# The end of a decoder block's FFN: the last token tile in two column pieces, its norm's sums in three parts

## The chip, the cores and the metric

One core of a Trainium2 chip runs the whole kernel in one launch. The metric is the device time in microseconds, median of three runs. TensorE multiplies, VectorE (DVE in the profile) and ScalarE (ACT) do the elementwise work, GpSimd (POOL) a part of it, and SyncE (SP) issues every DMA from one queue, in order.

## The reference, cut to what matters

One decoder layer on 1024 tokens and 16 meta tokens, model width 1024, in float32: a norm, a wide input projection, three mixers, a gated merge, a residual, a SwiGLU FFN of width 2816, a residual, and a final norm over each token.

```python
for l in range(DEPTH):
    u = rms_norm(h, norm_mix[l])
    proj = u @ w_in[l]
    ...
    g = jax.nn.sigmoid(gates).reshape(b, t, N_BRANCH, D_MODEL)
    merged = (g[:, :, 0] * (o_a @ w_branch[l, 0])
              + g[:, :, 1] * (o_f @ w_branch[l, 1])
              + g[:, :, 2] * (o_c @ w_branch[l, 2]))
    h = h + merged @ w_out[l]
    u = rms_norm(h, norm_ffn[l])
    gate_ff, up_ff = jnp.split(u @ w_ffn_in[l], 2, axis=-1)
    h = h + (jax.nn.silu(gate_ff) * up_ff) @ w_ffn_out[l]
return rms_norm(h, norm_final)[:, N_META:]
```

`rms_norm(y)` is y times the gain, divided by the root of the mean of y squared over the 1024 columns plus 1e-6.

## The kernel before, in words

Every product is made of three TensorE multiplies: an operand is split into a high and a low part, and high by high, high by low and low by high are summed in a PSUM bank. A full multiply moves 512 columns over a 128 by 128 weight tile.

The stages run in this order. The normalised input lies feature by feature in the four `u` tiles `uh0`, `ul0`, `uh1`, `ul1` (L210). The projections multiply weight tiles with them, and the mixers run in between. The 24 gate tiles (`gate`, L733) come from the same projections: for each of them TensorE makes two halves of 512 tokens, the second from `uh1` and `ul1`, ScalarE copies each half to a `z` tile, and a DMA writes that to DRAM (`gz`). The mixers' outputs lie in DRAM too (`osp`). After the last gate the `u` tiles are given up. The branch stage (L800 to L828) then multiplies the mixer outputs with the branch weights. It holds 24 tiles of 4096 bytes a partition, `oA`, `oC` and `oF` (all named `o4` in the program), loaded by `load_o` (L773). `oA` and `oC`, 16 tiles in the pool `r3`, are used first, in turns; `oF`, 8 tiles in the pool `b4`, is used only from L848 on. The branch weights (`wb`) and the gates (`sg`) are fetched two steps ahead (`fetch`, L777). Branch products are named `mm_br`, projections `mm_w`.

SBUF is filled from two sides. The pools `const`, `wstream` and `z` stand at the left side, in this order, and the `u` pool behind them; the pools of a stage stand at the right side. A tile that takes the place of an earlier one waits until the last reader of the earlier one is done. `const` is filled up with a `pad` of 192 bytes (L72) so that what follows starts at a multiple of 512 bytes. In the program as built, `ul1` takes the bytes 101888 to 118272 of each partition, and the first `oA` tile, `o4_1421`, starts at 118272.

Python code states the work; a scheduler then sets the order on each engine by a model of when things are ready, keeping what depends on what. TensorE runs its rows in order, and SP issues its DMAs in order: a DMA that waits holds back all that stand behind it.

The FFN's second product is cut into seven block products (a Strassen-like scheme, `product2(i, banks, ...)`, L1139), each over 11 operand pairs `ab` of 128 by 512, for four token tiles x of 128 tokens. The last one, `product2(6, yb, False, last)` at L1209, loads all 11 pairs and then goes token tile by token tile. After each tile, `last(x)` adds the PSUM bank to the residual `ho[4 + x][0]` (DVE), `total` squares and sums it (ACT, `Square` with an accumulator, into `sums`), and `finish` makes the reciprocal root (`rstd_from`, L176: a DVE `tensor_scalar` on the first column, an ACT `Sqrt` on the last one, a DVE reciprocal), multiplies both halves by it and by the gain `gfc` (DVE) and writes them out.

```python
def rstd_from(q, n):
    ...
    first = q[:n, 0:1]
    if q.shape[-1] > 2:
        tc.keep_in_program_order(dve.tensor_tensor(r[:n], first, q[:n, 1:2], ALU.add))
        first = r[:n]
    dve.tensor_scalar(e[:n], first, 1.0 / D, EPS, ALU.mult, ALU.add)
    act.activation(r[:n], q[:n, -1:], AF.Sqrt, bias=e[:n], scale=1.0 / D)
    dve.reciprocal(r[:n], r[:n])
```

Of the kernel before, what the change touches and what calls it, by code (L numbers as in the profile page):

```python
# [9 lines left out]
F32 = mybir.dt.float32  # L10
F32R = mybir.dt.float32r
AF = mybir.ActivationFunctionType
ALU = mybir.AluOpType
# [3 lines left out]
P = 128  # L17
# [34 lines left out]
def hybrid_block(ctx, tc, h_in, w_in, w_v0, w_v1, w_bd, par, rows, gains, relt, onehot,  # L52
                 maskrow, cmask, w_br, w_out, w_fi, w_fo, out):
    nc = tc.nc
    act, dve, pool, pe = nc.scalar, nc.vector, nc.gpsimd, nc.tensor

    def dma(dst, src):
        nc.sync.dma_start(f32(dst) if dst.dtype == F32R else dst, f32(src) if src.dtype == F32R else src)
# [7 lines left out]
    cp = ctx.enter_context(tc.tile_pool(name="const", bufs=1, side="left"))  # L66
# [12 lines left out]
    def nm(s):  # L79
        uid[0] += 1  # L80
        return f"{s}_{uid[0]}"
# [94 lines left out]
    def rstd_from(q, n):  # L176

        e = cp.tile([P, 1], F32, tag="re", bufs=4, name=nm("re"))
        r = cp.tile([P, 1], F32, tag="rs", bufs=4, name=nm("rs"))
# [7 lines that stand above are left out]
        return r  # L187

    def rstd_of(x, n, junk):

        q = cp.tile([P, 2], F32, tag="sq2", bufs=4, name=nm("sq"))
        for i in range(2):
            act.activation(junk[i], x[i], AF.Square, accum_out=q[:n, i:i + 1])
        return rstd_from(q, n)

    def halves(x):
        return x[:, :512], x[:, 512:]
# [633 lines left out]
    with tc.tile_pool(name="r4", bufs=1, side="right", reuse_waits="tile") as r4:  # L831
# [26 lines left out]
        with tc.tile_pool(name="r4b", bufs=1, side="right", reuse_waits="tile") as r4b:  # L858
            for c in range(2):
                u2[c] = [pair_tile(mp if c else bp) for k in range(KT // 2)]  # L860
                for tt in range(4 * c, 4 * c + 4):
# [3 lines left out]
                    q = slice(t0, t0 + P)  # L865
# [8 lines left out]
                    r = rstd_of(halves(ht), P, halves(xg))  # L874
# [20 lines left out]
    NJ = NF // 2  # L895
# [6 lines left out]
    def add(eng, o, a, b):  # L902
        eng.tensor_tensor(o, a, b, ALU.add)

    with tc.tile_pool(name="r5", bufs=1, side="right", reuse_waits="tile") as r5:
        def t5(tag, bufs, n=512):
            return r5.tile([P, n], F32, tag=tag, bufs=bufs, name=nm(tag))
# [6 lines left out]
        def operand(pl, tag, bufs, src):  # L914
            t = pl.tile([P, 2, 512], F32R, tag=tag, bufs=bufs, name=nm(tag))
            split(t[:, 0], t[:, 1], src)
            return t

        def swiglu_plain(f):
            w = [load_w(w_fi[f + NF * i], D) for i in range(2)]  # L920
            at_ = []
            for c in range(2):
                pg, pv = (mm_bank(f"_{x}{f}") for x in "gu")
                for ps, (wh, wl) in zip((pg, pv), w):
                    run(mm3(ps, [(wh[:, k * P:(k + 1) * P], wl[:, k * P:(k + 1) * P],
                                  u2[c][k // 2][0][:, k % 2], u2[c][k // 2][1][:, k % 2]) for k in range(KT)]))
                sg = t5("a", 6)
                act.activation(sg, pg, AF.Sigmoid)
                dve.tensor_tensor(sg, pg, sg, ALU.mult)
                dve.tensor_tensor(sg, pv, sg, ALU.mult)  # L930
                at_.append(sg)
            return at_

        def fetch_fi(f, i):
            w = []
            for s in range(2):
                pl = wp if i % 2 else r5
                raw = pl.tile([P, D], F32, tag="wr", bufs=2, name=nm("wr"))
                dma(raw, w_fi[f + NF * s])
                w.append(halves(raw))  # L940
            return w
# [124 lines left out]
        for j in range(NJ):  # L1066
            if j == 0:
                first, second = swiglu_plain(0), swiglu_plain(NJ)
                bb, last, rest = combine()
                spill(0, j, first[0])  # L1070
            elif j == 1:
# [3 lines left out]
                with behind(*last)():  # L1075
                    ops = [t5("s2", 2)] + [operand(r5, "ar", 3, a) for a in (a11, a12)]
# [8 lines left out]
                    ops = [t5("s2", 2), operand(wp, "wh", 2, a11), operand(wp, "wl", 2, a12)]  # L1085
# [7 lines left out]
                first = first_  # L1093
                spill(0, j, first[0])
                second, _ = swiglu(1 + NJ, w_, bb, None, ops, behind(*mark))
            else:
                with tc.issue_after(seen):
                    first, _ = swiglu(j, fetch_fi(j, 0), bb, pool)
# [13 lines left out]
    with (tc.tile_pool(name="ring0", bufs=4, side="right", reuse_waits="tile") as r7,  # L1112
          tc.tile_pool(name="ring1", bufs=10, side="right", reuse_waits="tile") as r8,
          tc.tile_pool(name="r6", bufs=1, side="right", reuse_waits="tile") as r6):
        def h_tile(tt, half):
            t = r6.tile([P, 512], F32, name=f"h{tt}{half}")
            dma(t, h1s[tt, :, 512 * half:512 * half + 512])
            return t

        def right_operand(i, j):  # L1120
            if i in bsp:
                return bsp[i][j]
            row, half = {0: (j, 0), 1: (j + NJ, 0), 5: (j + NJ, 1)}[i]
            return w_fo[row * P:(row + 1) * P, 512 * half:512 * half + 512]

        ring = [0]

        def operands(i, j):

            raw = wp.tile([P, 2, 512], F32, tag=("wr", "wh", "wl")[j % 3], bufs=2, name=nm("raw"))  # L1130
            dma(raw[:, 0], asp[i][j])
            dma(raw[:, 1], right_operand(i, j))
            pl = r7 if ring[0] % 14 < 4 else r8
            ring[0] += 1
            t = pl.tile([P, 2, 2, 512], F32R, tag="ab", name=nm("ab"))
            split(t[:, 0], t[:, 1], raw)
            return t[:, 0], t[:, 1]

        def product2(i, banks, first=True, by_token=None):  # L1139
            def mm(x, ops, js):  # L1140
                q = slice(x * P, (x + 1) * P)
                n = 3 * len(js)
                c = 0
                for j in js:
                    hi, lo = ops[j]
                    for a, b in ((hi, hi), (hi, lo), (lo, hi)):
                        pe.matmul(banks[x], a[:, 0, q], b[:, 1], start=first and j == 0 and c == 0,  # L1147
                                  stop=j == NJ - 1 and c % 3 == 2, skip_group_check=True)
                        c += 1
            if by_token is None:  # L1150
                for j in range(NJ):
                    ops = {j: operands(i, j)}
                    for x in range(4):
                        mm(x, ops, [j])
            else:
                ops = [operands(i, j) for j in range(NJ)]
                for x in range(4):
                    mm(x, ops, range(NJ))
                    by_token(x)

        xb = [mm_bank("_x0"), mm_bank("_x1"), mm_bank("_x2"), o_bank("_x3")]
        yb = [sc_bank("_y0"), sc_bank("_y1"), tr_bank("_y2"), tr_bank("_y3")]
        sums = cp.tile([P, 8, 2], F32, name="sums")

        def total(tt, half):

            o = ho[tt][half]
            junk = r6.tile([P, 512], F32, tag="jk", bufs=2, name=nm("jk"))
            act.activation(junk, o, AF.Square, accum_out=sums[:, tt, half:half + 1])

        def finish(tt):
            r = rstd_from(sums[:, tt], P)
            for half in range(2):
                sl = slice(512 * half, 512 * half + 512)
                o = ho[tt][half]
                dve.scalar_tensor_tensor(o, o, r, gfc[:, sl], ALU.mult, ALU.mult)
                dma(out[tt * P:(tt + 1) * P, sl], o)

        product2(0, yb)
        gfc = r6.tile([P, D], F32, name="gfc")  # L1180
        dma(gfc, gains[1:2].partition_broadcast(P))
        ho = [[h_tile(tt, half) for half in range(2)] for tt in range(8)]
        for x in range(4):
            add(dve, ho[x][0], yb[x], ho[x][0])
        product2(1, xb)
        for x in range(4):
            add(dve, ho[x][0], xb[x], ho[x][0])
            total(x, 0)
        product2(2, yb, False)
        for x in range(4):  # L1190
            add(dve, ho[x][1], yb[x], ho[x][1])
        product2(3, xb)
        for x in range(4):
            add(dve, ho[4 + x][1], xb[x], ho[4 + x][1])
        product2(4, yb, False)
        for x in range(4):
            add(dve, ho[4 + x][1], yb[x], ho[4 + x][1])
            total(4 + x, 1)
        product2(5, xb, False)
        for x in range(4):  # L1200
            add(dve, ho[x][1], xb[x], ho[x][1])
            total(x, 1)
            finish(x)

        def last(x):
            add(dve, ho[4 + x][0], yb[x], ho[4 + x][0])
            total(4 + x, 0)
            finish(4 + x)
        product2(6, yb, False, last)  # L1209

# [72 lines left out]
```

## Time and profile before

| | us |
|---|---|
| median of 3 runs | 1650.19 (1649.83 to 1652.05) |
| the profiled execution, its own time | 1652.01 |
| its span, first to last instruction | 1650.2 |
| TensorE busy | 1627.5 (99%) |
| VectorE busy | 1006.8 (61%) |
| ScalarE busy | 759.7 (46%) |
| GpSimd busy | 389.4 (24%) |
| granted TensorE clock, mean | 0.999 |

The profile shows one execution. Times count from the start of the span. A row of the timeline or of the chain of waits has the start, the duration, the engine, the line and what it works on; "xN" is the number of instructions that were merged. PEld is TensorE's weight load, SPq the queue of SP. Multiplies overlap in their pipeline, so the distance between starts tells their rate, not the duration of one.

### The profile page before, as it was taken

Reading aid. Unit: us, or ns where it says so; the run is one execution under the profiler, and the core shown is the slowest. Engines: PE = TensorE matmul, PEld = TensorE weight load, DVE = VectorE, ACT = ScalarE, POOL = GpSimd, SP = SyncE. Lnnn points to the kernel's source line nnn. Section 1 sums busy time; section 2 is a strip of 40 time slices with the busy share of each in tenths; the row PEclk is TensorE's granted clock in tenths of the full one; section 3 lists DMA queues with packets and bytes.
Section 4 is the critical chain, followed back from the end, with each engine's and each line's share of the span. In section 5 each row is a group of like instructions: output and inputs, shape, how many; then the busy total and the mean of one; then the engine's idle time right before and its main releaser. Section 6 shows DMA issues by size and latency. Waiting matters only on the chain.

```text
span 1650.2 us, 22634 instructions
## 1 busy us (share of the span) xinstructions
PE 1627.5 (99%) x8159; PEld 1372.3 (83%) x8159; DVE 1006.8 (61%) x1815; ACT 759.7 (46%) x1397; POOL 389.4 (24%) x322
## 2 busy tenths in 40 slices
PE   7999999999999999999999999999999999999998
PEld 6899978888888888888887888888888788888886
DVE  6566566555566666651338446977776777466554
ACT  6466466555555555542335443433333343355342
POOL 2000001011122221110224100267765667300000
PEclk9999999999999999999999999999999999999999
DMA  7222342223324142329747221344554444698632
GB/s 254 78 103 94 131 139 77 95 82 122 108 75 129 63 123 73 115 98 318 252 142 230 96 90 70 127 156 172 198 202 148 147 149 151 214 359 275 191 128 102
DMA packets 110880, 242.48 MB, mean 147 GB/s; under 512 B 11944, under 2 KB 23544, under 8 KB 110512
## 3 DMA queue, kind: packets, MB, share of 16 engines
q1 hardware_dynamic: 110768, 241.04, 43.0%
q8 instruction: 64, 1.05, 0.3%
q14 instruction: 48, 0.39, 0.1%
HBM read 163.45 MB, written 72.21 MB: 143 GB/s over the span
## 4 chain that ended last, share of the span: by engine, by line
PE 81%; DVE 6%; DMA 4%; POOL 3%; issue 3%; ACT 2%; SPq 0%; DVEq 0%; POOLq 0%; ACTq 0%
PE mm_w L151 27%; PE mm_s L151 7%; PE mm_br L151 6%; PE mm_wo L151 5%; PE mm_x L1147 4%; PE mm_v L151 4%; PE tr_s L151 4%; PE tr_y L1147 4%; PE sc_y L1147 4%; PE ob L547 4%; PE tr L558 3%; DMA wr<-w_fi_dram 2%; PE sc_s L151 2%; PE ob_x L1147 1%; PE mm_g L151 1%
## 5 line engine op out<-in xcount | busy, mean ns | idle before, releaser
L151 PE MATMUL mm_w<-uh,wh 128*128 128x512 f32 (+2 forms) x744 | 292.6, 393 | 0.0
L151 PE MATMUL mm_w<-uh,wl 128*128 128x512 f32 (+2 forms) x744 | 280.6, 377 | 0.0
L151 PE MATMUL mm_w<-ul,wh 128*128 128x512 f32 (+2 forms) x744 | 279.9, 376 | 0.0
L151 PEld LDWEIGHTS mm_w<-uh,wl 128*128 128x128 f32 x744 | 140.0, 188 | 25.7
L151 PEld LDWEIGHTS mm_w<-uh,wh 128*128 128x128 f32 x744 | 140.4, 189 | 12.8
L151 PEld LDWEIGHTS mm_w<-ul,wh 128*128 128x128 f32 x744 | 140.7, 189 | 11.7
L119 DVE TENSOR_TENSOR ab<-raw,ab 128x1024 fp32r<-128x1024 f32 x77 | 92.9, 1223 | 71.5 <-ACT ab L118 62.0
L118 ACT ACTIVATE wh<-wr 128x1024 fp32r<-128x1024 f32 (+1 forms) x84 | 72.0, 858 | 125.3 <-PE mm_w L151 52.3
L118 ACT ACTIVATE ab<-raw 128x1024 fp32r<-128x1024 f32 x77 | 80.8, 1059 | 95.0 <-PE ob_x L1147 21.4
L151 PE MATMUL mm_s<-pt,ar 128*128 128x512 f32 x492 | 118.8, 390 | 0.8 <-ACT c L954 0.7
L151 PE MATMUL mm_br<-o,wh 128*128 128x512 f32 x384 | 118.3, 389 | 0.0
L119 DVE TENSOR_TENSOR pl<-tr,ph 128x384 fp32r<-128x384 f32 (+2 forms) x160 | 87.4, 555 | 46.9 <-ACT ph L118 42.7
L151 PEld LDWEIGHTS mm_s<-pt,ar 128*128 128x128 f32 x492 | 92.0, 188 | 21.5 <-ACT c L968 1.3
L118 ACT ACTIVATE ph<-tr 128x384 fp32r<-128x384 f32 (+2 forms) x160 | 77.0, 486 | 52.9 <-PE tr L558 50.9
L119 DVE TENSOR_TENSOR wl<-wr,wh 128x1024 fp32r<-128x1024 f32 x45 | 55.8, 1241 | 73.4 <-ACT wh L118 73.1
L648 POOL TENSOR_SCALAR s<-s,sm 128x144 f32<-128x144 f32 (+3 forms) x64 | 48.8, 765 | 171.0 <-DVE sm L647 138.1
L151 PEld LDWEIGHTS mm_br<-o,wh 128*128 128x128 f32 x384 | 72.1, 188 | 14.8
L558 PE MATMUL tr<-ident,s 128*128 128x128 f32 x480 | 79.6, 274 | 1.2 <-POOL s L596 0.6
L151 PE MATMUL mm_wo<-woh,hl 128*128 128x512 f32 x256 | 79.1, 389 | 0.0
L151 PE MATMUL mm_br<-o,wl 128*128 128x512 f32 x192 | 75.2, 392 | 1.5 <-DVE wl L119 1.5
L558 PEld LDWEIGHTS tr<-ident,s 128*128 128x128 f32 x480 | 59.1, 140 | 18.3 <-DVE pl L119 3.4
L1147 PE MATMUL mm_x<-ab 128*128 128x512 f32 x297 | 72.7, 389 | 0.0
(258 smaller groups left out, 3651.9 us busy)
## 6 DMA issues: line engine op xcount, KB each, us to landing
wr<-w_in_dram SPq DMA_DIRECT2D x45, 512.0 KB, 3.6
wr<-w_fi_dram SPq DMA_DIRECT2D x44, 512.0 KB, 4.1
raw<-asp SPq DMA_DIRECT2D x77, 256.0 KB, 3.3
asp<-a SPq DMA_DIRECT2D x66, 256.0 KB, 2.8
gz<-z SPq DMA_DIRECT2D x48, 256.0 KB, 2.0
o<-osp SPq DMA_DIRECT2D x24, 512.0 KB, 5.9
sg<-gz SPq DMA_DIRECT2D x48, 256.0 KB, 3.5
fo<-w_fo_dram SPq DMA_DIRECT2D x22, 512.0 KB, 4.5
```

The source lines that it names most:

```text
L118: a = act.activation(hi, src, AF.Copy)
L119: i = dve.tensor_tensor(lo, src, f32(hi), ALU.subtract)
L151: pe.matmul(ps, a, b, start=first and i == 0, stop=i == n - 1, skip_group_check=not first)
L547: pe.matmul(ob[:, q0:q0 + b - a], vt[:, c], x[:, a:b], start=count == 0, stop=count == n_mm - 1, skip_group_check=True)
L558: pe.transpose(tb[:, col:col + P], src, ident)
L648: pool.tensor_scalar(s[:, :nk], s[:, :nk], den, 1.0, ALU.mult, ALU.mult)
L1147: pe.matmul(banks[x], a[:, 0, q], b[:, 1], start=first and j == 0 and c == 0, stop=j == NJ - 1 and c % 3 == 2, skip_group_check=True)
```

## The change

The last token tile (x = 3) of the last block product is made in two pieces of 256 columns: 33 multiplies for columns 0 to 255, then 33 for columns 256 to 511. `last` runs after each piece on its columns. The sums of squares of a token are kept in three columns of `sums` where two were: the half that was finished earlier, piece 0 (or the full tile for x < 3) and piece 1; the earlier half is now column 0, so that `tensor_scalar` no longer reads the last sum. For x = 3 the second half of the output is multiplied by the gain beforehand (`scaled`, a new tile and a DVE instruction before the last product) and then by the reciprocal root on ScalarE (`Copy` with a scale), while DVE does the first half.

```diff
-                    mm(x, ops, range(NJ))
-                    by_token(x)
+                    for cols in PIECES if x == 3 else ((0, 512),):
+                        mm(x, ops, range(NJ), slice(*cols))
+                        by_token(x, slice(*cols))
...
-        sums = cp.tile([P, 8, 2], F32, name="sums")
+        sums = cp.tile([P, 8, 3], F32, name="sums")
+        PIECES = ((0, 256), (256, 512))
...
-            act.activation(junk, o, AF.Square, accum_out=sums[:, tt, half:half + 1])
+            act.activation(junk[:, cols], o[:, cols], AF.Square, accum_out=sums[:, tt, i:i + 1])
...
-            r = rstd_from(sums[:, tt], P)
+            r = rstd_from(sums[:, tt, :2 if scaled is None else 3], P)
...
-                dve.scalar_tensor_tensor(o, o, r, gfc[:, sl], ALU.mult, ALU.mult)
+                if half and scaled is not None:
+                    o = scaled
+                    act.activation(o, o, AF.Copy, scale=r)
+                else:
+                    dve.scalar_tensor_tensor(o, o, r, gfc[:, sl], ALU.mult, ALU.mult)
...
+        scaled = r6.tile([P, 512], F32, name="scaled")
+        dve.tensor_tensor(scaled, ho[7][1], gfc[:, 512:], ALU.mult)
```

`sums` lies in the pool `const`. It grows from 64 to 96 bytes a partition, and every left pool behind it moves by 32 bytes: in the program as built, `ul1` now takes 101920 to 118304, while `o4_1421` still starts at 118272. The two share 32 bytes.

The rows of SP between the mixers and the branch stage change with it. `z_1397` to `z_1420` are the halves of the last gates, `wr_1414` the last projection weights, `o4_1421` to `o4_1436` `oA` and `oC`, `o4_1437` to `o4_1444` `oF`, `wor` weights of the output product. Before, SP has there, from the last projection weights on:

```order
L58 DMA wr_1414_7761<-w_in_dram 128x1024
L58 DMA o4_1421_7836<-osp_94 128x1024
L58 DMA gz_92<-z_1397_7606 128x512
L58 DMA o4_1425_7840<-osp_94 128x1024
L58 DMA o4_1422_7837<-osp_94 128x1024
L58 DMA o4_1426_7841<-osp_94 128x1024
L58 DMA gz_92<-z_1399_7634 128x512
```

The first tile of `oA` stands right behind the last projection weights, and the others follow among the writes of the gates; the sixteenth, `o4_1436`, and the first branch weights, `wb_1445`, stand ahead of the write of `z_1418`. Now SP has at the same place:

```order
L58 DMA wr_1414_7761<-w_in_dram 128x1024
L58 DMA o4_1437_7852<-osp_94 128x1024
L58 DMA gz_92<-z_1397_7606 128x512
L58 DMA o4_1441_7856<-osp_94 128x1024
L58 DMA o4_1438_7853<-osp_94 128x1024
L58 DMA o4_1442_7857<-osp_94 128x1024
L58 DMA gz_92<-z_1399_7634 128x512
```

The tiles of `oF` have moved to where `oA` was. `oA` now stands around the last two writes of the gates:

```order
L58 DMA gz_92<-z_1413_7758 128x512
L58 DMA gz_92<-z_1418_7792 128x512
L58 DMA o4_1421_7836<-osp_94 128x1024
L58 DMA gz_92<-z_1420_7820 128x512
L58 DMA o4_1425_7840<-osp_94 128x1024
L58 DMA o4_1422_7837<-osp_94 128x1024
L58 DMA o4_1426_7841<-osp_94 128x1024
```

All 16 tiles of `oA` and `oC` have moved behind the write of `z_1418`, and 15 of them behind that of the very last half, `z_1420`. The branch weights follow them directly, here with the last three tiles of `oC` (`o4_1435`, `o4_1432`, `o4_1436`):

```order
L58 DMA o4_1435_7850<-osp_94 128x1024
L58 DMA o4_1432_7847<-osp_94 128x1024
L58 DMA o4_1436_7851<-osp_94 128x1024
L58 DMA wb_1445_7876<-w_br_dram 128x512
L58 DMA sg_1446_7878<-gz_92 128x512
L58 DMA sg_1447_7879<-gz_92 128x512
```

The weights have moved with the tiles: nothing of the branch stage's first step is ahead of `z_1418` any more. TensorE's and DVE's rows between the mixers and the branch stage are the same in both.

At the end of the program ScalarE now has, from the third token tile's sum on (`jk` is scrap, `rs` the reciprocal root, `h70` and `scaled` the two halves of the last tile):

```order
L1172 ACTIVATE jk_2373_14510,sums_13011<-h60_13236 128x512
L185 ACTIVATE rs_2375_14513<-sums_13011,re_2374_14512 128x1
L1172 ACTIVATE jk_2376_14555,sums_13011<-h70_13240 128x256
L1172 ACTIVATE jk_2377_14591,sums_13011<-h70_13240 128x256
L185 ACTIVATE rs_2379_14594<-sums_13011,re_2378_14593 128x1
L1181 ACTIVATE scaled_14318<-scaled_14318,rs_2379_14594 128x512
```

Where one sum of 512 columns stood, two of 256 stand, and the scaling of the second half is last; no table load stands among them.

More of the change, by code (lines that the diff above doesn't have):

```diff
@@ L1139, in product2, with mm @@
         def product2(i, banks, first=True, by_token=None):
-            def mm(x, ops, js):
+            def mm(x, ops, js, cols=slice(0, 512)):
                 q = slice(x * P, (x + 1) * P)
@@ L1146, in mm @@
                     for a, b in ((hi, hi), (hi, lo), (lo, hi)):
-                        pe.matmul(banks[x], a[:, 0, q], b[:, 1], start=first and j == 0 and c == 0,
+                        pe.matmul(banks[x][:, cols], a[:, 0, q], b[:, 1, cols], start=first and j == 0 and c == 0,
                                   stop=j == NJ - 1 and c % 3 == 2, skip_group_check=True)
@@ L1157, in product2, with total, finish @@
                 for x in range(4):
-                    mm(x, ops, range(NJ))
-                    by_token(x)
+                    for cols in PIECES if x == 3 else ((0, 512),):
+                        mm(x, ops, range(NJ), slice(*cols))
+                        by_token(x, slice(*cols))
         xb = [mm_bank("_x0"), mm_bank("_x1"), mm_bank("_x2"), o_bank("_x3")]
         yb = [sc_bank("_y0"), sc_bank("_y1"), tr_bank("_y2"), tr_bank("_y3")]
-        sums = cp.tile([P, 8, 2], F32, name="sums")
-        def total(tt, half):
+        sums = cp.tile([P, 8, 3], F32, name="sums")
+        PIECES = ((0, 256), (256, 512))
+        def total(tt, half, i, cols=slice(0, 512)):
             o = ho[tt][half]
             junk = r6.tile([P, 512], F32, tag="jk", bufs=2, name=nm("jk"))
-            act.activation(junk, o, AF.Square, accum_out=sums[:, tt, half:half + 1])
-        def finish(tt):
-            r = rstd_from(sums[:, tt], P)
+            act.activation(junk[:, cols], o[:, cols], AF.Square, accum_out=sums[:, tt, i:i + 1])
+        def finish(tt, scaled=None):
+            r = rstd_from(sums[:, tt, :2 if scaled is None else 3], P)
             for half in range(2):
@@ L1187, in hybrid_block @@
             add(dve, ho[x][0], xb[x], ho[x][0])
-            total(x, 0)
+            total(x, 0, 0)
         product2(2, yb, False)
@@ L1197, in hybrid_block @@
             add(dve, ho[4 + x][1], yb[x], ho[4 + x][1])
-            total(4 + x, 1)
+            total(4 + x, 1, 0)
         product2(5, xb, False)
@@ L1201, in hybrid_block, with last @@
             add(dve, ho[x][1], xb[x], ho[x][1])
-            total(x, 1)
+            total(x, 1, 1)
             finish(x)
[L1205 to L1208, printed above, removed]
+        scaled = r6.tile([P, 512], F32, name="scaled")
+        dve.tensor_tensor(scaled, ho[7][1], gfc[:, 512:], ALU.mult)
+        def last(x, cols):
+            add(dve, ho[4 + x][0][:, cols], yb[x][:, cols], ho[4 + x][0][:, cols])
+            total(4 + x, 0, 2 if cols.start else 1, cols)
+            if cols.stop == 512:
+                finish(4 + x, scaled if x == 3 else None)
         product2(6, yb, False, last)
```

## The prediction

> **What bounds the kernel now.** The page's busy times come first.
>
> ```profile
> PE 1627.5 (99%) x8159; PEld 1372.3 (83%) x8159; DVE 1006.8 (61%) x1815; ACT 759.7 (46%) x1397; POOL 389.4 (24%) x322
> ```
>
> TensorE is busy for 99% of the span, so a microsecond is won where TensorE isn't running, and lost where it is made to wait. The change is aimed at the stretch behind TensorE's last multiply. The timeline from 1643.4 us on:
>
> ```profile
> 1643.48 0.69 DVE L903 TENSOR_TENSOR h<-tr_y,h 128x512 f32<-128x512 f32 x1 [3.81 <-PE tr_y L1147]
> 1644.26 0.63 ACT L1169 ACTIVATE jk<-h 128x512 f32<-128x512 f32 x1 [6.24 <-DVE h L903]
> 1644.80 0.19 ACT L1169 ACTIVATION_READ_ACCUMULATOR jk<-h 128x1 f32 x1
> 1645.02 0.15 DVE L184 TENSOR_SCALAR re<-sums 128x1 f32<-128x1 f32 x1 [0.85 <-ACT jk L1169]
> 1645.21 0.29 ACT L185 ACTIVATE rs<-sums,re 128x1 f32<-128x1 f32 x1 [0.22 <-DVE re L184]
> 1645.53 0.16 DVE L186 RECIPROCAL rs<-rs 128x1 f32<-128x1 f32 x1 [0.36 <-ACT rs L185]
> 1645.73 1.42 DVE L1176 SCALAR_TENSOR_TENSOR h<-h,rs,gfc 128x512 f32<-128x512 f32 x2
> 1646.51 0.99 SPq L58 DMA_DIRECT2D out_dram<-h  x2
> ```
>
> It is one chain: add, square, offset, root, reciprocal, two scalings, two writes. From 1643.48 to the span's end are 6.7 us; that is all that the end can ever give. The order rows show a second place, the start of the branch stage, so I read the chain of waits there:
>
> ```profile
> 732.52 0.96 PE ob L547 x8
> ...
> 734.41 42.88 PE mm_w L151 x189
> 777.30 86.83 PE mm_br L151 x383
> ```
>
> The last projections (`mm_w`) go over into the first branch products (`mm_br`) at 777.30 without a gap, 383 of them without a wait. The SP queue's timeline shows why:
>
> ```profile
> 738.03 0.40 SPq L58 DMA_DIRECT2D o<-osp  x1
> ...
> 767.49 0.43 SPq L58 DMA_DIRECT2D o<-osp  x1
> 767.97 0.44 SPq L58 DMA_DIRECT2D wb<-w_br_dram  x1
> ```
>
> Between the first and the last of these `o` rows lie all 16 tiles of `oA` and `oC`, and the first branch weights follow at 767.97. ScalarE has those at 774.37, 2.9 us before they are needed:
>
> ```profile
> 774.37 0.63 ACT L118 ACTIVATE wh<-wb 128x512 fp32r<-128x512 f32 x1 [1.83 <-DMA wb<-w_br_dram]
> ```
>
> **The start of the branch stage, where I expect the change to be decided.** `sums` is 32 bytes larger, and `ul1` now overlaps `o4_1421`. That tile's load must wait for the last reader of `ul1`, the last `mm_w`, done at 777.30. In SP's order the other 15 loads, `wb_1445` and the gates' `sg` stand behind it, so nothing of the first step is in SBUF when TensorE wants to begin. TensorE's own rows are unchanged: `mm_br` is next, and nothing can fill the gap. The sizes:
>
> ```profile
> gz<-z SPq DMA_DIRECT2D x48, 256.0 KB, 2.0
> o<-osp SPq DMA_DIRECT2D x24, 512.0 KB, 5.9
> ...
> wb<-w_br_dram SPq DMA_DIRECT2D x24, 256.0 KB, 3.6
> ```
>
> From 777.30 to the first weights, 16 x 512 KB, the last gate write of 256 KB and 256 KB of weights go through: 8.5 MiB, 8.91 MB. For the rate I have the window in which the same loads ran before, and the densest run of loads, 13 of 256 KB (3.41 MB):
>
> ```profile
> 738.00:748.00 10.00, 10.00 (x46) 8.29 (x45) 1.23 (x1) 2.14 (x3) 0.00 (x0) 1.00 0.97 345
> ```
>
> ```profile
> 1444.18 8.44 SPq L58 DMA_DIRECT2D h<-h1s  x13
> ```
>
> The first gives 345 GB/s at a DMA share of 0.97, so 356 at a full share; the second 3.41 MB in 8.44 us, 404 GB/s. I take 356, since it is the same tiles: 25.0 us. The ends are 22.1 us (404) and 27.9 us (320, some 7% under the row, for gate reads in between). [...]
>
> To this come the landing of a transfer in an empty queue, 2.0 us by the `gz` row, and after the weights' landing ScalarE's `wh` (0.63 us by its row) and the weight load (0.19 by the row below), with some 0.05 of semaphores: 2.9 us. So `mm_br` begins at 777.30 + 25.0 + 2.9 = 805.2. Before, by the distance of 0.23 between multiplies, the first began at about 777.1: a delay of 28.1 us. What covered these loads before was 39 us of projections (738.03 to 777.30); what runs under them now is nothing.
>
> Does TensorE resume at full speed? The start of the kernel shows how it behaves after idling:
>
> ```profile
> 9.28 1.94 PE L205 MATMUL tr<-ident,xg 128*128 128x128 f32 x8 [9.28 <-DVE xg L302]
> ...
> 18.21 0.43 PE L151 MATMUL mm_w<-uh,x0h 128*128 128x272 f32 x1
> 18.44 0.43 PE L151 MATMUL mm_w<-ul,x0h 128*128 128x272 f32 x1
> ...
> 19.62 0.29 PE L151 MATMUL mm_w<-ul,x0h 128*128 128x272 f32 x1
> 19.75 0.28 PE L151 MATMUL mm_w<-uh,x0l 128*128 128x272 f32 x1
> ```
>
> ```profile
> 15.68 5.10 PE mm_w L151 x25
> ```
>
> ```profile
> 16.00:18.00 2.00, 2.00 (x10) 1.77 (x10) 1.13 (x4) 1.97 (x5) 1.57 (x1) 1.00 0.82 246
> ```
>
> The granted clock reads 1.00 throughout, yet equal multiplies stand 0.23 us apart until about 19.4 and 0.125 apart after it. By the clock column resuming costs nothing; by the spacing, 3.8 us of dense work (15.68 to about 19.5) lose 45%, 1.7 us. I take 1.7; ends 0 and 4.5 (10 us, counted from 9.28). [...]
>
> Of this delay little can come back, since TensorE hardly waits later in this stage:
>
> ```profile
> PE mm_br L151 <- DVE wl L119: 1.5, 4, 0.6
> ```
>
> At most 1.5 us; I take 0. That `oF` and `wor` come earlier costs nothing: they take `oA`'s old places, with fewer bytes.
>
> **The end.** Terms, by form:
>
> ```profile
> L118 ACT ACTIVATE ph<-tr 128x512 fp32r<-128x512 f32 x64 | 38.0, 594 | 17.5 <-PE tr L558 16.1 <-ACT z L736 0.7
> ...
> L118 ACT ACTIVATE ph<-tr 128x256 fp32r<-128x256 f32 x32 | 12.2, 380 | 18.6 <-PE tr L558 18.5
> ```
>
> ```profile
> L119 DVE TENSOR_TENSOR pl<-tr,ph 128x256 fp32r<-128x256 f32 x32 | 13.5, 423 | 7.8 <-ACT ph L118 4.5 <-DMA osp<-pl 2.6
> ```
>
> ```profile
> L547 PEld LDWEIGHTS ob<-ph,v 128*128 128x128 f32 x272 | 51.2, 188 | 6.7 <-ACT ph L118 1.8
> ```
>
> - The pieces: 66 multiplies of 256 columns with a weight load each; the eight `ob` of that size above took 0.96, 0.12 each: 7.92 us against 33 x 0.227 (86.83/383) = 7.48. +0.44.
> - The add on 256 columns: 0.42 against 0.69. -0.27.
> - `Square`: ScalarE saves 594 - 380 ns from 512 to 256 columns. -0.21.
> - The offset's row (1645.02 to 1645.21) leaves the path. -0.19. Its two small DVE steps run under the last `Square` and its read (some 0.6 us); without that cover they cost 2 x 0.17, gaps included.
> - Both halves are scaled at once. The second write was issued at 1647.17 (1646.51 + 0.99 - 0.33), 1.48 after the reciprocal's end; now ScalarE is done some 0.69 after it, its write takes 0.33, and the other stands behind: 1.06. -0.42.
>
> Together -0.65, between -1.2 and, if none of the shortened steps helps, +0.5. The added gain product is one more DVE step while DVE is 61% busy; it hides under the last product.
>
> **The sum.** 28.1 + 1.7 - 0.65 = 29.1 us on the span of 1650.2. The profiled execution took 1652.01, its span 1650.2; the median of 1650.19 equals the span, so I put the sum on it: 1679.3. Least: 22.1 for 25.0, no slow clock, 1.5 back, -1.2 at the end: 1672.7. Most: 27.9, 4.5, +0.5: 1686.1.
>
> **The rivals.**
> - *The loads are hidden anyway*, and only the end counts: 1649.5, so not slower. It decides if the 16 loads are issued before 777.3 - 27.9 = 749.4. For it: before, SP had the last one out at 767.5. Against: the order rows put 15 behind the write of `z_1420`, which the last `mm_w` feeds. 0.05.
> - *The shift by 32 bytes slows transfers as well.* The stream tiles no longer start at multiples of 512 bytes. [...] No row before shows a shifted stream tile. 0.05.
> - *The pieces are bound by their weight loads*: 66 x 0.188 = 12.4, 4.5 more: 1683.8. Against it the eight `ob`, with equal loads, at 0.12. 0.02.
> - *The end isn't shortened* (ScalarE's scaling comes late): 1680.0. 0.03.
>
> **How the numbers follow.** My forecast has 0.85, at 1679.3. The last three rivals lie in its range; only the first falls out. I give 1673 to 1686. A measurement can tell about 0.2%, 3.3 us: the first rival is "same", 0.05; faster needs more than the end saves, 0.01; slower 0.94.
>
> **What would show it.** TensorE idle from 777.3 to about 805, ended by ScalarE's `wh` behind `wb`; `o` loads at 777 to 790; slow multiplies for some 4 us after that; then the old pace. At the end, 7.9 us for the last tile and writes 1.06 us after the reciprocal. A gap under 20 us, or none, would prove me wrong.

## The result and the profile after

The changed kernel takes 1690.14 us (median, 1688.43 to 1692.74) beside 1650.05 us for the kernel before (four runs of each): a ratio of 1.0236, 95% interval 1.0221 to 1.0251, or 40.1 us more. The prediction had 1679.3, with a range up to 1686: the direction and the place were right, the size was not. The profiled execution took 1689.88 us, its span 1688.1; the mean granted clock fell from 0.999 to 0.991. The two spans differ by 37.9 us, less than the medians, since the profiled execution of the kernel before took 1652.01 us, more than its median.

I read the profile in the order of the prediction. The branch stage first; the chain of waits there, around the one large gap:

```profile
734.05 42.90 PE mm_w L151 x189
777.02 0.61 ACT z L736
777.65 0.32 SPq L58
...
782.35 10.20 DMA o<-osp
792.57 9.37 DMA wb<-w_br_dram
802.02 0.64 ACT wh L118
802.70 91.38 PE mm_br L151 x383
```

The projections no longer go over into the branch products. The chain leaves TensorE at 777.02, goes through ScalarE's last gate half, SP, the loads of `o` and the first branch weights, and comes back at 802.70. SP's timeline shows the loads where the order rows had put them, one ahead of the last gate write and 15 behind it, and that write waits for ScalarE's copy:

```profile
776.74 0.32 SPq L58 DMA_DIRECT2D o<-osp  x1
777.65 0.32 SPq L58 DMA_DIRECT2D gz<-z  x1
778.02 13.62 SPq L58 DMA_DIRECT2D o<-osp  x15
792.57 0.33 SPq L58 DMA_DIRECT2D wb<-w_br_dram  x1
```

The list of waits gives the price, in total, number of times and longest:

```profile
PE mm_br L151 <- ACT wh L118: 25.8, 1, 25.8
```

And the windows of the gap (busy times of the five engines, then the granted clock, the DMA share and the rate) show nothing but DMA, at up to 420 GB/s, until TensorE resumes in the third:

```profile
778.00:788.00 10.00, 0.00 (x0) 0.00 (x0) 0.00 (x0) 0.00 (x0) 0.00 (x0) 0.56 0.95 354
788.00:798.00 10.00, 0.00 (x0) 0.00 (x0) 0.00 (x0) 0.00 (x0) 0.00 (x0) 0.50 1.03 420
798.00:808.00 10.00, 5.30 (x15) 4.22 (x16) 1.85 (x3) 4.62 (x7) 0.00 (x0) 0.57 0.91 331
```

So far the prediction holds. What it did not hold is in the row of the chain that starts at 802.70: the same 383 multiplies that took 86.83 us take 91.38, and the slow clock explains only 1.9 of the 4.5 (below). In the FFN, 300 us after the gap, the groups of 12 multiplies stand in the chain like this:

```profile
1104.42 2.80 PE sc_s L151 x12
1107.23 2.80 PE mm_s L151 x12
1110.02 2.80 PE tr_s L151 x12
```

In the kernel before such a group stood there like this:

```profile
1052.71 2.72 PE sc_s L151 x12
```

That is 12 x 0.2267. At 2.80 it is 0.2333 us a multiply, and TensorE waits for nobody there. That is the first thing the prediction had no term for.

The second is at the end, in the timeline from the second piece on:

```profile
1677.32 4.21 PE L1147 MATMUL tr_y<-ab 128*128 128x256 f32 x33 [0.52 <-DVE h L903]
...
1681.56 0.42 DVE L903 TENSOR_TENSOR h<-tr_y,h 128x256 f32<-128x256 f32 x1 [4.30 <-PE tr_y L1147]
...
1682.02 0.42 ACT L1172 ACTIVATE jk<-h 128x256 f32<-128x256 f32 x1 [4.21 <-DVE h L903]
...
1682.89 0.17 DVE L186 RECIPROCAL rs<-rs 128x1 f32<-128x1 f32 x1 [0.65 <-ACT rs L185]
1683.09 0.72 ACT L1181 ACTIVATE scaled<-scaled,rs 128x512 f32<-128x512 f32 x1 [0.23 <-DVE rs L186]
1683.09 0.75 DVE L1183 SCALAR_TENSOR_TENSOR h<-h,rs,gfc 128x512 f32<-128x512 f32 x1
1683.84 0.33 SPq L58 DMA_DIRECT2D out_dram<-scaled  x1
1684.59 0.33 SPq L58 DMA_DIRECT2D out_dram<-h  x1
```

The second piece waits 0.52 us for DVE's addition of the first one. From the last multiply to the reciprocal it is then 0.72 us shorter than before (from the last multiply's end to the reciprocal's, 1.53 beside 2.25).

### The profile page after: what moved, and what is told of

It reads as the page before. It is cut to its first block, busy times and chain, and to the rows that moved or that the text cites. A ratio compares the mean times of both kernels' runs of the same rounds, so it can differ in the third digit from the quotient of the medians.

```text
span 1688.1 us, 22691 instructions
## 1 busy us (share of the span) xinstructions
PE 1641.6 (97%) x8192; PEld 1375.9 (82%) x8192; DVE 979.3 (58%) x1817; ACT 763.5 (45%) x1400; POOL 384.7 (23%) x322
## 4 chain that ended last, share of the span: by engine, by line
PE 90%; DVE 3%; ACT 2%; DMA 2%; issue 1%; SPq 0%; POOL 0%; ACTq 0%; DVEq 0%; POOLq 0%
PE mm_w L151 27%; PE mm_s L151 13%; PE tr_s L151 7%; PE mm_br L151 6%; PE mm_wo L151 5%; PE mm_x L1147 4%; PE mm_v L151 4%; PE tr_y L1147 4%; PE sc_y L1147 4%; PE sc_s L151 3%; PE ob L547 3%; PE tr L558 3%; PE ob_x L1147 1%; PE mm_g L151 1%; PE mm_u L151 1%
## 5 line engine op out<-in xcount | busy, mean ns | idle before, releaser
L151 PEld LDWEIGHTS mm_w<-uh,wh 128*128 128x128 f32 x744 | 140.4, 189 | 12.8
L151 PEld LDWEIGHTS mm_w<-ul,wh 128*128 128x128 f32 x744 | 140.7, 189 | 11.8
L151 PE MATMUL mm_br<-o,wh 128*128 128x512 f32 x384 | 122.2, 400 | 25.8 <-ACT wh L118 25.8
```

Of the source, the lines that this page charges most:

```text
L151: pe.matmul(ps, a, b, start=first and i == 0, stop=i == n - 1, skip_group_check=not first)
```

## The experiments

Three theories went in. **T1** is the prediction's sum: stall, cold clock (TensorE's slow multiplies right after it has idled), then the old pace. **T2** is what the trace suggests: besides those, a multiply is slower where its two operands lie in tiles of which only one has moved by 32 bytes (left-hand pools moved, right-hand pools did not), and the end loses by the wait between the pieces. **T3** is the rival for the pace: the idle stretch or its low clock leaves TensorE slower for the rest of the run, whatever the addresses.

### The end alone

```diff
 (the changed kernel)
-    pad(cp, 192)
+    pad(cp, 160)
```

> The changed kernel with its left-hand pools 32 bytes lower (the filler of const 160 instead of 192 bytes), so that every pool behind const lies where it lay before the change: no overlap, no moved loads, and what is left of the change is its end. T1 (the prediction's sum: the stall and the cold clock, then the old pace, and an end of -0.65) expects 1649.4 us. T2 (the stall, the cold clock, a slower pace wherever one operand of a multiply lies 32 bytes off the other, and an end that loses because the second piece waits for the addition of the first) expects the trace's end again: second piece 0.5 us after the first, 8.7 instead of 7.5 us for the twelve-times-two multiplies and more of the last token tile, 0.7 us less from the last multiply to the reciprocal; +0.5 us, or 1.0 if the last write again lands late: 1650.6 to 1651.1. T3 (the slower pace is a lasting trace of the idle stretch or of its clock, whatever the addresses) says of this run what T2 says.

Measured: 1651.12 us, ratio 1.0006 [0.9997, 1.0016], so 0.9 us more, and no difference is within the interval. The gap at the branch stage is gone. By the total alone T1's 1649.4 lies just outside; the trace decides. Its chain ahead of the end and the end's wait:

```profile
1611.21 14.96 PE sc_y L1147 x66
1626.17 11.44 PE tr_y L1147 x66
1637.64 0.43 DVE h L903
1638.12 4.22 PE tr_y L1147 x33
```

```profile
PE tr_y L1147 <- DVE h L903: 0.5, 1, 0.5
```

In the kernel before:

```profile
1613.52 14.96 PE sc_y L1147 x66
1628.48 14.97 PE tr_y L1147 x66
```

So the pieces end 31.14 us after the start of the last `sc_y` multiplies (1611.21 to 1642.35), where the kernel before took 29.94 (1613.52 to 1643.46): +1.20. From the last multiply's end to the span's end it is 5.95 instead of 6.74: 0.79 come back. T2's account of the end stands: +0.4 by the trace. What follows from this run is more than that: with 32 bytes taken from a filler, nearly all of the 40 us is gone.

### The stall alone

```diff
 (the kernel before)
-    with tc.tile_pool(name="r3", bufs=16, side="right", reuse_waits="tile") as r3:
+    with (tc.tile_pool(name="gap", bufs=1, side="right") as gap,
+          tc.tile_pool(name="r3", bufs=16, side="right", reuse_waits="tile") as r3):
+        gap.tile([P, 128], F32, name="gap512")
```

> The kernel before with a 512-byte filler ahead of the pool r3 of the branch stage: its last tile of o comes to overlap the end of ul, as in the changed kernel, and SP's loads stand in the changed kernel's order, but every operand keeps its place within 512 bytes. T1 and T2: stall 25.6 and cold clock 1.9 as the trace of the changed kernel has them, 1677.6 us (1676.5 to 1679), and behind the first ten or so multiplies of the branch stage a multiply each 0.2267 us, 383 of mm_br in about 88.8 us. T3: the slow pace comes with the idle stretch, so 0.2333 us a multiply and some 9.5 us more, about 1687.

Measured: 1678.76 us, ratio 1.0177 [1.0163, 1.0191], 28.6 us more. The waits and the chain:

```profile
PE mm_br L151 <- ACT wh L118: 27.0, 1, 27.0
```

```profile
803.16 88.98 PE mm_br L151 x383
...
965.54 10.91 PE mm_wo L151 x48
```

The kernel before has the same groups of `mm_wo`:

```profile
949.47 10.91 PE mm_wo L151 x48
```

After the same idle stretch the multiplies are back at 10.91 us for 48, the pace of before. T3 falls: it wanted 1687 and 11.2. The prediction's own term, 29.8 for the stall and the cold clock together, is borne out.

TensorE's timeline of this run shows the cold clock without the other effect:

```profile
803.16 1.22 PE L151 MATMUL mm_br<-o,wh 128*128 128x512 f32 x2 [27.02 <-ACT wh L118]
...
807.15 0.63 PE L151 MATMUL mm_br<-o,wh 128*128 128x512 f32 x2
```

Nine multiplies start from 803.16 on before the one at 807.15: 3.99 us instead of 9 x 0.227 = 2.04, so 1.95 us are lost. From there on the distance is 0.23.

### The offset alone

```diff
 (the kernel before)
-    pad(cp, 192)
+    pad(cp, 160)
```

> The kernel before with its left-hand pools 32 bytes lower (filler 160 instead of 192 bytes), the right-hand pools as they were: no overlap, the same order on all engines, only the two operands of many multiplies 32 bytes off each other. T2: 6.7 ns more for each multiply of mm_br, mm_wo and of those FFN products with one operand on either side, some 9.5 us in all, 1659.5 us (1657 to 1663; the small constants move too, the identity of the transposes among them, which they did not in the changed kernel); 12 multiplies of sc_s take 2.80 instead of 2.72 us. T1 and T3: no idle stretch, no slower pace, 1650.0 us.

Measured: 1661.10 us, ratio 1.0070 [1.0055, 1.0085], 10.9 us more, with no gap anywhere. T1 and T3 fall. The chain:

```profile
776.75 89.38 PE mm_br L151 x383
...
964.57 11.20 PE mm_wo L151 x48
...
1076.58 2.80 PE sc_s L151 x12
```

The 383 branch products take 2.55 us longer without any cold clock, 6.7 ns each, and 48 of `mm_wo` take 11.20 instead of 10.91, as in the changed kernel.

### Both sides moved

```diff
 (the kernel before)
-    pad(edge, LINE - 32)
-    pad(cp, 192)
+    pad(edge, LINE)
+    pad(cp, 160)
```

> As the run before, but the right-hand pools 32 bytes lower as well (filler of edge 512 instead of 480 bytes): every tile of SBUF lies 32 bytes off its old place, and no operand lies off another. T2, if it is the offset between the two operands that costs: 1650.0 us and 0.2267 us a multiply. T4 (the rival within T2: a tile that starts off a multiple of 64 bytes is read more slowly, whatever the other operand does): at least the 1659.5 of the run before, and more, since then both operands of every multiply are off. T1 and T3: 1650.0.

Measured: 1649.92 us, ratio 0.9997 [0.9986, 1.0007].

```profile
974.77 10.91 PE mm_wo L151 x48
...
1073.13 2.72 PE sc_s L151 x12
```

The old pace, though no tile stands where it stood. T4, the absolute address, falls. It is the place of one operand against the other that costs.

### The 32 bytes without the change

```diff
 (the kernel before)
         sums = cp.tile([P, 8, 2], F32, name="sums")
+        cp.tile([P, 8], F32, name="more")
```

> The kernel before with one unused tile of 32 bytes a partition behind sums: the end as before, the places of all pools and the order on all engines as in the changed kernel. T2 adds the runs with one of the two alone: 28.6 us of the run with the stall alone and 10.9 of the run with the offset alone, less about 1 us, since in the trace of the changed kernel the slower pace was worth some 9.5: 1688.6 to 1689.7 us. T1 (the stall with the cold clock is all that 32 bytes do): 1678.8. A rival that the two share something (the slower multiplies hide part of the late loads): clearly under 1688.

Measured: 1689.95 us, ratio 1.0243 [1.0229, 1.0257]: 40.2 us more beside 1649.71 in its comparison. An unused tile of 32 bytes a partition makes the whole loss. T1 falls again; the stall alone (28.6) and the offset alone (10.9) add up to 39.5, so the two share nothing that these runs can see.

### How far apart: 64, 128 and 256 bytes

```diff
 (the kernel before; one run each)
-    pad(cp, 192)
+    pad(cp, 128)
...
-    pad(edge, LINE - 32)
+    pad(edge, LINE - 32 - 128)
...
-    pad(edge, LINE - 32)
+    pad(edge, LINE - 32 - 256)
```

> The kernel before with its left-hand pools 64 bytes lower (filler 128 instead of 192 bytes) and the right-hand pools as they were, the order the same: operands 64 bytes off each other instead of 32. If any offset within 512 bytes costs what 32 did: 1661 us and 2.80 us for twelve multiplies of sc_s. If places are told apart only within 64 bytes: 1650.2 us and 2.72. In between, if the cost goes by the offset's size.

> The kernel before with its right-hand pools 128 bytes higher (filler of edge 352 instead of 480 bytes), the left-hand pools as they were, the order the same: the two operands of the mixed multiplies lie 128 bytes off each other. With 32 bytes such a multiply took 6.6 ns more than 226.8, with 64 bytes 2.4 ns (weights below the moving rows) or 6.2 (above them). If the cost falls with the distance, 128 bytes cost less than 64 did: under 1656 us, near 1650 if it is gone. If every place other than the same one within 512 bytes costs: 1655 to 1661.

> The same with 256 bytes (filler of edge 224). Falling with the distance: 1650.0 us and 226.8 ns a multiply. Any place but the same within 512 bytes: 1655 to 1661.

Measured: 64 bytes 1656.06 us, ratio 1.0037 [1.0023, 1.0050]; 128 bytes 1659.97 us beside 1648.09, 1.0071 [1.0054, 1.0088]; 256 bytes 1648.09, 1.0000 [0.9990, 1.0009]. The groups by line show it per multiply, mean ns of one, here of `mm_br`, for 64, 128 and 256 bytes in turn:

```profile
L151 PE MATMUL mm_br<-o,wh 128*128 128x512 f32 x384 | 119.1, 391 | 0.0
```

```profile
L151 PE MATMUL mm_br<-o,wh 128*128 128x512 f32 x384 | 120.6, 395 | 0.0
```

```profile
L151 PE MATMUL mm_br<-o,wh 128*128 128x512 f32 x384 | 118.4, 389 | 0.0
```

It was 389 before. To see both directions I sorted the multiplies of 512 columns behind 820 us by the place of the next multiply's weights against the moving rows of this one, modulo 512 bytes (places from the built program, starts from the traces), and took the mean distance to the next start, in ns, with the count:

| run | same place | weights above by | weights below by |
|---|---|---|---|
| before | 226.9 (3527) | - | - |
| both sides moved | 226.8 (3544) | - | - |
| 32 bytes | 227.4 (1761) | 233.1 (482) | 233.4 (1302) |
| 64 bytes | 227.2 (1761) | 233.0 (482) | 229.2 (1303) |
| 128 bytes | 227.0 (1761) | 233.2 (482) | 232.9 (1304) |
| 256 bytes | 226.7 (1759) | 226.9 (1774), either | |

For 64 bytes alone a cost that goes by the distance would fit; with all three runs neither of the two expectations does. The cost doesn't fall with the distance (128 bytes cost as much as 32), and not every place costs (256 bytes cost nothing). Of the places tried, the same one and the one 256 bytes away are free; at 64 bytes the weights above cost 6.2 ns and the weights below 2.4. That this is the direction isn't shown, since the two groups are also different multiplies (the ones above are nearly all `mm_s` and `tr_s` with `ar`). Nor is it shown that the next multiply's weights count rather than the same one's own: sorted by its own weights the means are the same within 0.1 ns, and at the borders where the two sortings differ, the multiplies of the 32-byte run are slow by either (20 `mm_s` with only the next weights off take 234.6 ns, 19 `sc_s` with only their own off 233.3). Why the place costs is open.

### The piece ahead of another tile

```diff
 (the end alone)
-                for x in range(4):
-                    for cols in PIECES if x == 3 else ((0, 512),):
-                        mm(x, ops, range(NJ), slice(*cols))
-                        by_token(x, slice(*cols))
+                for x, cols in ((0, (0, 512)), (1, (0, 512)), (3, PIECES[0]), (2, (0, 512)), (3, PIECES[1])):
+                    mm(x, ops, range(NJ), slice(*cols))
+                    by_token(x, slice(*cols))
```

> The changed kernel with the left-hand pools back in place, and the first 256 columns of the last token tile multiplied ahead of the third token tile: their addition then runs beside the third tile's 33 multiplies, and the second piece follows those. If the 0.5 us between the pieces is PE waiting for the addition of the first (T2), the second piece starts 0.02 us after the third tile's last multiply and the time falls by 0.5 us from the run with the end alone, to 1650.6. If the wait comes from something else on the way (T1's sum had none), it stays, 1651.1.

Measured: 1649.18 us, ratio 0.9998 [0.9989, 1.0007]. The chain of the end:

```profile
1610.66 14.96 PE sc_y L1147 x66
1625.62 15.42 PE tr_y L1147 x99
...
1641.06 0.44 DVE h L903
```

The total can't tell 1650.6 from 1651.1; the chain can. All 99 multiplies of `tr_y` run in one piece of it; the wait is gone. From the start of `sc_y` to the last multiply's end it is 30.38 us, beside 31.14 with the wait and 29.94 before. So the wait was DVE's addition, and it cost 0.76: 0.5 of waiting, and 0.26 because the second piece then took 4.22 instead of 3.96.

### Only the scaling on ScalarE

```diff
 (the kernel before)
+                if half and scaled is not None:
+                    o = scaled
+                    act.activation(o, o, AF.Copy, scale=r)
+                    act.dma_start(out[tt * P:(tt + 1) * P, sl], o)
+                else:
...
+        scaled = r6.tile([P, 512], F32, name="scaled")
+        dve.tensor_tensor(scaled, ho[7][1], gfc[:, 512:], ALU.mult)
```

> The kernel before with only the last step changed: no pieces, the second half of the last token tile scaled on ScalarE, which also issues that half's write from its own queue. By the trace of the run with the end alone, ScalarE's scaling takes 0.72 us beside VectorE's 0.75, so both writes start 0.8 us after the reciprocal instead of 0.8 and 1.5 as before: 0.6 to 0.7 us less, 1649.5. The rival: a write issued by ScalarE starts or lands later than one of SP's, which no run has shown so far; then nothing is gained or up to 2 us are lost.

Measured: 1649.49 us, ratio 0.9994 [0.9982, 1.0005]. The writes do start together, 0.8 us after the reciprocal:

```profile
1640.89 0.72 ACT L1178 ACTIVATE scaled<-scaled,rs 128x512 f32<-128x512 f32 x1 [0.23 <-DVE rs L186]
1640.89 0.75 DVE L1181 SCALAR_TENSOR_TENSOR h<-h,rs,gfc 128x512 f32<-128x512 f32 x1
1641.64 0.40 ACTq L1179 DMA_DIRECT2D out_dram<-scaled  x1
1641.67 0.33 SPq L58 DMA_DIRECT2D out_dram<-h  x1
```

The total, at 0.2 us less with an interval of 3.0 less to 0.8 more, can't show a gain of 0.6. By the trace there is none: the span ends at 1645.3, 3.7 us after the first of them. Before it ended at 1650.2, also 3.7 us after its first write at 1646.51, though the second came 0.66 later; with the end alone 3.7 (1644.64 to 1648.3) with 0.43 in between. All nine traces without the idle stretch have 3.65 to 3.76 us. In these runs the distance from the first write to the end doesn't depend on when the second is issued, so starting the second earlier gains nothing. Neither expectation has it: by the trace nothing is gained, but not because ScalarE's write starts late.

## Why the prediction was wrong, step by step

| step | predicted, us | measured, us |
|---|---|---|
| branch stage starts late | 28.1 | 25.9 in the changed kernel, 27.2 with the stall alone |
| cold clock | 1.7 | 1.95 |
| given back later | 0 | at most 0.7 (TensorE's other waits behind 780 us: 2.5 before, 1.8 with the stall alone) |
| every later step at the old pace | 0 | 10.9 |
| the end | -0.65 | +0.4 by the trace with the end alone, +1.0 in the changed kernel |
| sum | 29.1 | 40.1 by the medians; the rows, with the changed kernel's figures where there are two, add up to 39.1 to 39.8 |

- **The late start** was right in cause, place and kind. From the first `mm_w` of the last projections to the first `mm_br` it is 802.70 - 734.05 = 68.65 us, before 777.1 - 734.41 = 42.7: 25.9 more (with the stall alone 803.16 - 733.26 = 69.9, 27.2 more). The 28.1 came out too long because the loads with their landing took 25.0 us (777.02 to 802.02) and not 27.0: I put the rate at 356 GB/s throughout, and the second window ran at 420. A term the other way was missing: 15 of the loads also stood behind ScalarE's copy of the last gate half and its write, and went out from 778.02 on.
- **The cold clock** was right in kind and nearly in size: 1.95 by the stall-alone run's nine slow multiplies, and this time the granted clock shows it too: in the changed kernel it reads 0.50 in the windows from 780 to 806 us and 1.00 again from 807 on.
- **"Then the old pace" is the step that failed.** I let the tiles' shift touch the allocation (the overlap) and, as a rival, the transfers, but not TensorE itself. I had no row of it: before, every pair of operands of this part of the kernel lies at the same place within 512 bytes. The runs put 10.9 us in its place (9.1 to 14.0 by the interval). By the spacing it is 12.8: 1969 multiplies from 777 us on, 6.5 ns each; TensorE's wait for DVE in the branch stage falls from 1.5 to 0.5 and gives 1.0 back, which leaves 11.8, inside that interval. What in the hardware makes the place matter was not shown.
- **Transfers slowed by the shift**, the second rival, did not show. In the offset-alone run TensorE's list of waits behind 780 us has one entry, 0.5 us for DVE, and none for a transfer:

```profile
PE mm_br L151 <- DVE wl L119: 0.5, 1, 0.5
```

- **The end** has two wrong terms. The pieces cost +1.20, not +0.44: the second waits for the addition of the first, on other columns of the same PSUM bank; in the program as built its first multiply waits for a DVE semaphore. I looked only at what runs behind the last multiply. That wait is 0.52 us in the trace, and the prediction had no term for it. And the scaling of both halves at once gives about 0, not -0.42, since the end follows the first write. In the changed kernel the second write even went out 1.53 us behind the reciprocal, where I had 1.06 and the kernel before 1.48. The three terms of the chain from the last multiply to the reciprocal, -0.67 together, were right (-0.72).
- In the changed kernel the end is another 0.6 us longer than with the end alone, since the span ends 4.3 us behind the first write (1683.84 to 1688.1) instead of 3.7. The two other runs with the stall show the same (4.2 in both) and no run without it does. In these three the second write went out 0.75 us behind the first, later than in any other run; whether that is the link is open, since no run tried it.

So the loss is not in what the change does but in where its 32 bytes lie: 28.6 + 10.9 = 39.5 of some 40 us. The version with the filler adapted and the first piece ahead of the third tile is the best that these runs point to. By the trace its end is 0.34 us shorter than before (30.38 + 5.96 from the start of the last `sc_y` multiplies to the span's end, beside 29.94 + 6.74); by the medians it can't be told from the kernel before.

## What to carry to other kernels

A tile that grows moves everything allocated behind it, so compare the built addresses before reading the edit's own arithmetic: an overlap of a few bytes can turn a prefetch into a wait (32 bytes and 25.9 us here), and an offset between the two operands can be paid on every multiply: some 6.5 ns on 227 here. Where TensorE is the bound, keep weights and moving rows at the same place within 512 bytes or 256 bytes apart, the two found free here (226.7 to 227.4 ns a multiply), and take a new tile's bytes out of a filler. A column piece of a bank isn't free of the other piece's reader (0.52 us of waiting here); put other multiplies in between, as in the run with the piece ahead of another tile, where TensorE waited for nothing at the end.

## What was unexpected of the hardware

- A multiply of 512 float32 columns takes 226.8 ns from start to start when weights and moving rows lie at the same place or 256 bytes apart (226.7 to 227.4 by run), 233.1 to 233.4 when they are 32 bytes apart, 232.9 to 233.2 at 128, and 229.2 or 233.0 at 64, in two groups of multiplies. With both sides moved by 32 bytes it is 226.8.
- The loads into SBUF, the last of 512 KB and the first of 256 KB, ran at 420 GB/s from 788 to 798 us with TensorE idle, in the changed kernel and with the stall alone.
- With two writes of 256 KB last, the span ended 3.65 to 3.76 us after the first one's issue, whether the second came 0.03, 0.43 or 0.66 us behind it. In the three runs with the stall, where it came 0.75 us behind, it was 4.24 to 4.26.
